# RMSNorm in float32: statistics one group ahead, scaling shared between three engines

## The chip, the cores and the metric

The kernel runs on one core of a Trainium2 chip. The metric is the device time of one execution in microseconds (us). Before the change the median of 12 runs is 162.3 us (162.03 to 162.85).

## What is computed

```python
def setup_inputs():
    batch, seq, dim = 16, 1024, 512
    return {"x": np.random.randn(batch, seq, dim).astype(np.float32),
            "gamma": np.ones(dim, dtype=np.float32)}

def reference(x, gamma):
    eps = 1e-5
    rms = np.sqrt(np.mean(x ** 2, axis=-1, keepdims=True) + eps)
    return (x / rms * gamma).astype(np.float32)
```

There are 16,384 rows of 512 floats. Each row is divided by the root of its mean square and multiplied by gamma. The input is 33.55 MB and the output as much, so 67.1 MB pass between HBM and the on-chip memory, each byte once.

## The kernel before

The rows are cut into four tiles (t = 0 to 3) of 128 partitions x 32 rows. One partition's share of a tile is 32 rows in succession, 64 KB. Three slots in SBUF, `slots[0..2]`, each hold a tile; tile 3 uses slot 0 again. A row is scaled in its slot and stored from there.

All loads and stores are issued from SP, in the order in which the program gives them (lines 47 to 49 and 96 to 116). An issue whose wait is not over holds every later one. The order is written out by hand: the first tile as two loads of 16 rows, tile 1 as one load of 32; then, once the first rows are scaled, three stores of a single row (rows 0, 1 and 2 of tile 0), with loads of 16, 8 and 8 rows of tile 2 between them; then the store of rows 3 to 31 of tile 0; the first half of tile 1; the two loads of tile 3, which need slot 0 to be stored; the second half of tile 1; tile 2 whole; and tile 3 in two halves.

`compute(slot, r0, r1)` (line 64) goes over groups of G = 8 rows. Sums of squares come in two ways, in turn:

- In even groups ACT squares one row at a time (line 78) and gives the row's sum through its accumulator, eight instructions for a group.
- In odd groups ACT squares H = 4 rows at a time into a PSUM tile `sq` (line 72; the pool has two buffers), and DVE reduces it to four sums (line 73), twice for a group.

Then ACT takes the root, with the mean and eps folded in (line 84), DVE the reciprocal (line 85), and DVE scales the eight rows one by one with a SCALAR_TENSOR_TENSOR, row x rstd x gamma (line 87). All four engines run their own queues in order; Tile's scheduler places independent instructions of different groups between each other on each engine. GpSimd (POOL) does nothing but four small memsets. Gamma is spread over the partitions at the start by a matmul with a column of ones into PSUM (line 56), and copied to SBUF as `gamma_b` (line 58).

Of the kernel before, what the change touches and what calls it, by code (L numbers as in the profile page):

```python
# [1 line left out]

# [4 lines left out]


@with_exitstack
def kernel(  # L10
    ctx: ExitStack,
    tc: tile.TileContext,
    x: bass.AP,
    gamma: bass.AP,
    out: bass.AP,
):
    nc = tc.nc
    P = nc.NUM_PARTITIONS
    eps = 1e-5
    fp32 = mybir.dt.float32  # L20
    AF = mybir.ActivationFunctionType
    OP = mybir.AluOpType

    xf = x.flatten_outer_dims()
    of = out.flatten_outer_dims()
    N, D = xf.shape
    R = 32
    G = 8
    H = 4
    assert N == 4 * P * R  # L30

    xv = xf.rearrange("(t p r) d -> t p r d", p=P, r=R)
    ov = of.rearrange("(t p r) d -> t p r d", p=P, r=R)

    const = ctx.enter_context(tc.tile_pool(name="const", bufs=1))
    stats = ctx.enter_context(tc.tile_pool(name="stats", bufs=4))
    psum = ctx.enter_context(tc.tile_pool(name="psum", bufs=2, space=bass.MemoryType.PSUM))

    slots = [const.tile([P, R, D], fp32, name=f"slot{i}") for i in range(3)]

    def load(t, slot, r0, r1):
        nc.sync.dma_start(out=slots[slot][:, r0:r1], in_=xv[t][:, r0:r1])

    def store(t, slot, r0, r1):
        nc.sync.dma_start(out=ov[t][:, r0:r1], in_=slots[slot][:, r0:r1])

    load(0, 0, 0, 16)
    load(0, 0, 16, 32)
    load(1, 1, 0, 32)

    gamma_row = const.tile([1, D], fp32)
    nc.scalar.dma_start(out=gamma_row, in_=gamma.unsqueeze(0))
    ones_col = const.tile([1, P], fp32)
    nc.vector.memset(ones_col, 1.0)  # L54
    gamma_psum = psum.tile([P, H, D], fp32, name="sq")
    nc.tensor.matmul(gamma_psum[:, 0], ones_col, gamma_row, start=True, stop=True)  # L56
    gamma_b = const.tile([P, D], fp32)
    nc.vector.tensor_copy(out=gamma_b, in_=gamma_psum[:, 0])  # L58

    eps_t = const.tile([P, 1], fp32)  # L60
    nc.vector.memset(eps_t, eps)  # L61
    sq_scratch = const.tile([P, D], fp32)

    def compute(slot, r0, r1):
        for g in range(r0, r1, G):
            ss = stats.tile([P, G], fp32, name="ss")
            rms = stats.tile([P, G], fp32, name="rms")
            rstd = stats.tile([P, G], fp32, name="rstd")
            if (g // G) % 2:
                for h in range(0, G, H):  # L70
                    sq = psum.tile([P, H, D], fp32, name="sq")
                    nc.scalar.activation(out=sq, in_=slots[slot][:, g + h : g + h + H, :], func=AF.Square)  # L72
                    nc.vector.tensor_reduce(  # L73
                        out=ss[:, h : h + H], in_=sq, axis=mybir.AxisListType.X, op=OP.add
                    )
            else:
                for r in range(G):
                    nc.scalar.activation(  # L78
                        out=sq_scratch,
                        in_=slots[slot][:, g + r, :],  # L80
                        func=AF.Square,
                        accum_out=ss[:, r : r + 1],
                    )
            nc.scalar.activation(out=rms, in_=ss, func=AF.Sqrt, bias=eps_t, scale=1.0 / D)  # L84
            nc.vector.reciprocal(out=rstd, in_=rms)  # L85
            for r in range(G):
                nc.vector.scalar_tensor_tensor(  # L87
                    out=slots[slot][:, g + r, :],
                    in0=slots[slot][:, g + r, :],
                    scalar=rstd[:, r : r + 1],  # L90
                    in1=gamma_b,
                    op0=OP.mult,
                    op1=OP.mult,
                )

    compute(0, 0, 8)
    store(0, 0, 0, 1)
    load(2, 2, 0, 16)
    store(0, 0, 1, 2)
    load(2, 2, 16, 24)  # L100
    store(0, 0, 2, 3)
    load(2, 2, 24, 32)
    compute(0, 8, 32)
    store(0, 0, 3, 32)
    compute(1, 0, 16)
    store(1, 1, 0, 16)
    load(3, 0, 0, 16)
    load(3, 0, 16, 32)
    compute(1, 16, 32)
    store(1, 1, 16, 32)  # L110
    compute(2, 0, 32)
    store(2, 2, 0, 32)
    compute(0, 0, 16)
    store(3, 0, 0, 16)
    compute(0, 16, 32)
    store(3, 0, 16, 32)


# [1 line left out]
_INS = ['x', 'gamma']  # L120
_OUTS = [((16, 1024, 512), 'float32')]


# [23 lines left out]
```

## Time and profile before

| | us |
|---|---|
| median of 12 runs | 162.3 (162.03 to 162.85) |
| the profiled execution, its own time | 162.34 |
| its span (first to last instruction in the profile) | 160.6 |
| DVE busy | 123.3 (77%), 163 instructions |
| ACT busy | 79.8 (50%), 162 records |
| POOL busy | 0.2 |
| mean transfer rate over the span | 418 GB/s (33.56 MB read, 33.55 MB written) |

Stores were issued from SP at 24.8 us (the first single row), 50.1 (rest of tile 0), 75.1 (first half of tile 1), 132.4 and 147.7 (the halves of tile 3). The loads of tile 3 were issued at 82.0 and 82.4, and landed 19.2 and 28.8 us later.

How to read the views. The page divides the span into 40 slices and gives the busy share of each engine in tenths, and the share of the 16 DMA engines. A table by stage gives, for each stretch, each engine's busy time, the number of its instructions in brackets, the clock, the share of the DMA engines and what they moved; a packet is counted whole in the stretch in which it starts, so a share can stand above 1.00 in a short one. A group of instructions carries its line in the kernel, engine, operation, tiles and shapes, count, then busy time in us and the mean of one in ns, then the idle time before it and what ended it. The list of waits gives who waited for what: us in total, times, longest. In the list of DMA queues, q1 is the queue of SP's loads and stores, q10 that of ACT's load of gamma, and q14 brings instructions; columns are packets, MB and the share of 16 engines' time.

### The profile page before, as it was taken

How to read it: one execution, taken by the hardware profiler on the slowest of the kernel's cores; microseconds unless marked ns; L12 is line 12 of the kernel's file. 1: busy time of each engine (PE TensorE's matmuls, PEld its weight loads, DVE VectorE, ACT ScalarE, POOL GpSimd, SP SyncE). 2: the span in 40 equal slices, each digit the busy share in tenths (PEclk: the TensorE clock that was granted, in tenths of full speed). 3: DMA queues.
4: the chain of work that ended last, by engine and by line, in shares of the span. 5: the costliest groups of instructions: out<-in, count | busy, mean ns of one | idle time of the engine just before them, and what ended most of it. 6: DMA issues, size and time to landing. Idle time of an engine off the chain costs nothing.

```text
span 160.6 us, 414 instructions
## 1 busy us (share of the span) xinstructions
PE 2.0 (1%) x2; PEld 0.5 (0%) x2; DVE 123.3 (77%) x163; ACT 79.8 (50%) x162; POOL 0.2 (0%) x4
## 2 busy tenths in 40 slices
PE   4000000000000000000000000000000000000000
PEld 1000000000000000000000000000000000000000
DVE  0101909999999509999999999998999999998000
ACT  3008999930490999999500934003998960000000
POOL 0000000000000000000000000000000000000000
DMA  7999999969799999998899999999999799799993
GB/s 262 392 400 506 400 408 506 522 261 522 327 394 404 441 445 514 461 459 370 370 441 457 408 425 473 400 433 465 408 514 457 343 506 457 335 392 400 506 400 139
DMA packets 2452, 67.13 MB, mean 418 GB/s; under 512 B 273, under 2 KB 273, under 8 KB 658
## 3 DMA queue, kind: packets, MB, share of 16 engines
q1 hardware_dynamic: 2448, 67.11, 97.7%
q14 instruction: 2, 0.02, 0.0%
q10 hardware_dynamic: 2, 0.00, 0.0%
HBM read 33.56 MB, written 33.55 MB: 418 GB/s over the span
## 4 chain that ended last, share of the span: by engine, by line
DVE 70%; ACT 12%; DMA 8%; issue 2%; DVEq 0%
DVE slot L87 51%; DVE ss L73 18%; DMA slot<-in_x_dram 8%; ACT sq_scratch L78 6%; ACT sq L72 4%; DVE rstd L85 1%; ACT L84 1%; ACT rms L84 1%; DVEq L142 0%
## 5 line engine op out<-in xcount | busy, mean ns | idle before, releaser
L87 DVE SCALAR_TENSOR_TENSOR slot<-slot,rstd,gamma_b 128x512 f32<-128x512 f32 x128 | 85.7, 743 | 0.1
L78 ACT ACTIVATE sq_scratch<-slot 128x512 f32<-128x512 f32 x64 | 40.0, 625 | 14.3 <-DMA slot<-in_x_dram 13.0
L73 DVE TENSOR_REDUCE ss<-sq 128x4 f32<-128x2048 f32 x16 | 36.1, 2268 | 10.3 <-ACT sq L72 10.2
L72 ACT ACTIVATE sq<-slot 128x2048 f32<-128x2048 f32 x16 | 29.8, 1861 | 13.9 <-DVE ss L73 13.9
L84 ACT ACTIVATE rms<-ss,eps_t 128x8 f32<-128x8 f32 x16 | 4.5, 297 | 28.0 <-DVE ss L73 27.7
L78 ACT ACTIVATION_READ_ACCUMULATOR sq_scratch<-slot 128x1 f32 x64 | 11.9, 186 | 0.0
L85 DVE RECIPROCAL rstd<-rms 128x8 f32<-128x8 f32 x16 | 2.9, 190 | 9.8 <-ACT rms L84 9.8
L58 DVE COPY gamma_b<-sq 128x512 f32<-128x512 f32 x1 | 0.7, 692 | 3.4 <-PE sq L56 3.4
L56 PE MATMUL sq<-gamma_row,ones_col 1*128 1x512 f32 x2 | 2.0, 1120 | 2.3 <-DMA gamma_row<-in_gamma_dram 2.3
L78 ACT ACT_TABLE_LOAD x1 | 1.3, 1283 | 1.3 <-PEq L131 1.3
L84 ACT ACT_TABLE_LOAD x1 | 1.3, 1283 | 0.0
L54 DVE MEMSET ones_col<- 1x128 f32 x1 | 0.2, 165 | 0.8 <-PEq L131 0.8
L56 PEld LDWEIGHTS sq<-gamma_row,ones_col 1*128 1x128 f32 x2 | 0.5, 304 | 2.3 <-issue 2.3
L131 POOL MEMSET const-bfloat16-1.0<- 128x1 bf16 x1 | 0.1, 103 | 0.0
L131 POOL MEMSET const-uint8-127<- 128x1 uint8 x1 | 0.1, 103 | 0.0
L131 POOL MEMSET const-float32-1.0<- 128x1 f32 x1 | 0.1, 100 | 0.0
L131 POOL MEMSET const-float32-0.0<- 128x1 f32 x1 | 0.1, 99 | 0.2 <-issue 0.2
L61 DVE MEMSET eps_t<- 128x1 f32 x1 | 0.1, 59 | 0.0
## 6 DMA issues: line engine op xcount, KB each, us to landing
slot<-in_x_dram SPq DMA_DIRECT2D x5, 4096.0 KB, 21.4
out_dram<-slot SPq DMA_DIRECT2D x4, 4096.0 KB, 16.5
out_dram<-slot SPq DMA_DIRECT2D x1, 7424.0 KB, 31.8
slot<-in_x_dram SPq DMA_DIRECT2D x2, 2048.0 KB, 34.6
out_dram<-slot SPq DMA_DIRECT2D x3, 256.0 KB, 23.0
gamma_row<-in_gamma_dram ACTq DMA_DIRECT2D x1, 2.0 KB
slot<-in_x_dram SPq DMA_DIRECT2D x1, 40.6
out_dram<-slot SPq DMA_DIRECT2D x1, 23.3
```

The costliest lines, as they stand in the source:

```text
L54: nc.vector.memset(ones_col, 1.0)
L56: nc.tensor.matmul(gamma_psum[:, 0], ones_col, gamma_row, start=True, stop=True)
L58: nc.vector.tensor_copy(out=gamma_b, in_=gamma_psum[:, 0])
L61: nc.vector.memset(eps_t, eps)
L72: nc.scalar.activation(out=sq, in_=slots[slot][:, g + h : g + h + H, :], func=AF.Square)
L73: nc.vector.tensor_reduce(out=ss[:, h : h + H], in_=sq, axis=mybir.AxisListType.X, op=OP.add)
L78: nc.scalar.activation(out=sq_scratch, in_=slots[slot][:, g + r, :], func=AF.Square, accum_out=ss[:, r : r + 1],)
L84: nc.scalar.activation(out=rms, in_=ss, func=AF.Sqrt, bias=eps_t, scale=1.0 / D)
L85: nc.vector.reciprocal(out=rstd, in_=rms)
L87: nc.vector.scalar_tensor_tensor(out=slots[slot][:, g + r, :], in0=slots[slot][:, g + r, :], scalar=rstd[:, r : r + 1], in1=gamma_b, op0=O ...
L131: nc = _bacc.Bacc("TRN2", target_bir_lowering=False, num_devices=1)
```

## The change

- The sums of all groups are made in one way: ACT squares four rows at a time, the first four of a group into PSUM (`sq0`), the last four into SBUF (`sq4`), one buffer each; DVE reduces both (`sum_squares`).
- The sums of group k + 1 are written in the program ahead of the scaling of group k (`apply`), and its root and reciprocal (`inverse_rms`) behind it.
- Scaling is shared. ACT scales the first four rows of a group by rstd with a Copy each; POOL then multiplies the four by gamma in one TENSOR_TENSOR of 128x2048. DVE scales the last four as before, but takes gamma from PSUM (`gamma_psum`) in place of SBUF.
- The first load, 16 rows, becomes two of 8 rows. All other transfers are issued in the same order; they stand in `transfers`, called behind each group.
- At the start, ACT and DVE get an `addr_align(128, offset=60, max_nops=0)`: the instruction that follows is placed at slot 60 of a stretch of 128 instruction slots, and the padding is branched over.

In the order of instructions on the engines: DVE has 64 SCALAR_TENSOR_TENSOR in place of 128, and 32 TENSOR_REDUCE in place of 16; ACT has 32 Squares, 64 Copies and 16 roots in place of 64 + 16 Squares and 16 roots; POOL has 16 TENSOR_TENSOR, and one more ISA instruction ahead of them (a reload of library code). On SP there is one issue more.

```diff
+    nc.scalar.addr_align(128, offset=60, max_nops=0)
+    nc.vector.addr_align(128, offset=60, max_nops=0)
...
-    psum = ctx.enter_context(tc.tile_pool(name="psum", bufs=2, space=bass.MemoryType.PSUM))
+    psum = ctx.enter_context(tc.tile_pool(name="psum", bufs=1, space=bass.MemoryType.PSUM))
...
-    load(0, 0, 0, 16)
+    load(0, 0, 0, 8)
+    load(0, 0, 8, 16)
...
-    gamma_psum = psum.tile([P, H, D], fp32, name="sq")
-    nc.tensor.matmul(gamma_psum[:, 0], ones_col, gamma_row, start=True, stop=True)
-    gamma_b = const.tile([P, D], fp32)
-    nc.vector.tensor_copy(out=gamma_b, in_=gamma_psum[:, 0])
+    gamma_psum = psum.tile([P, D], fp32, name="gamma_psum")
+    nc.tensor.matmul(gamma_psum, ones_col, gamma_row, start=True, stop=True)
+    gamma_b = const.tile([P, 1, D], fp32)
+    nc.vector.tensor_copy(out=gamma_b[:, 0], in_=gamma_psum)
...
-    sq_scratch = const.tile([P, D], fp32)
-    def compute(slot, r0, r1):
...
+    def sum_squares(slot, g):
+        ss = stats.tile([P, G], fp32, name="ss")
+        for h, home in ((0, psum), (H, const)):
+            sq = home.tile([P, H, D], fp32, name=f"sq{h}")
+            nc.scalar.activation(out=sq, in_=slots[slot][:, g + h : g + h + H, :], func=AF.Square)
+            nc.vector.tensor_reduce(out=ss[:, h : h + H], in_=sq, axis=mybir.AxisListType.X, op=OP.add)
+        return ss
+    def inverse_rms(ss):
+        rms = stats.tile([P, G], fp32, name="rms")
+        rstd = stats.tile([P, G], fp32, name="rstd")
+        nc.scalar.activation(out=rms, in_=ss, func=AF.Sqrt, bias=eps_t, scale=1.0 / D)
+        nc.vector.reciprocal(out=rstd, in_=rms)
+        return rstd
+    def apply(slot, g, rstd):
+        x = slots[slot]
+        for r in range(H):
+            nc.scalar.activation(
+                out=x[:, g + r, :], in_=x[:, g + r, :], func=AF.Copy, scale=rstd[:, r : r + 1]
+            )
+        nc.gpsimd.tensor_tensor(
+            out=x[:, g : g + H, :],
+            in0=x[:, g : g + H, :],
+            in1=gamma_b.to_broadcast([P, H, D]),
+            op=OP.mult,
+        )
+        for r in range(H, G):
+            nc.vector.scalar_tensor_tensor(
+                out=x[:, g + r, :],
+                in0=x[:, g + r, :],
+                scalar=rstd[:, r : r + 1],
+                in1=gamma_psum,
+                op0=OP.mult,
+                op1=OP.mult,
+            )
+    groups = [(t, g) for t in range(4) for g in range(0, R, G)]
+    slot_of = [0, 1, 2, 0]
+    def transfers(t, g):
...
+        elif (t, g) == (0, 24):
+            store(0, 0, 3, 32)
+        elif (t, g) == (1, 8):
+            store(1, 1, 0, 16)
+            load(3, 0, 0, 16)
+            load(3, 0, 16, 32)
...
+    rstd = inverse_rms(sum_squares(0, 0))
+    for k, (t, g) in enumerate(groups):
+        more = k + 1 < len(groups)
+        if more:
+            tn, gn = groups[k + 1]
+            ss = sum_squares(slot_of[tn], gn)
+        apply(slot_of[t], g, rstd)
+        if more:
+            rstd = inverse_rms(ss)
+        transfers(t, g)
```

## The prediction

> **What bounds the kernel now.** I read the page's share lines first: which resource is full, not which engine is busiest.
>
> ```profile
> span 160.6 us, 414 instructions
> ...
> DMA  7999999969799999998899999999999799799993
> ...
> q1 hardware_dynamic: 2448, 67.11, 97.7%
> q14 instruction: 2, 0.02, 0.0%
> ...
> DVE 70%; ACT 12%; DMA 8%; issue 2%; DVEq 0%
> ```
>
> The queue of loads and stores keeps 16 DMA engines at work for 97.7% of 160.6 us, 156.9 us. The chain of waits names DVE at 70%; that is a trap. It follows whoever released the last store, and says nothing of whether the transfers were idle meanwhile. The stage table tells that:
>
> ```profile
> core 0: us, PE busy (x) PEld busy (x) DVE busy (x) ACT busy (x) POOL busy (x), PEclk, DMA share, GB/s
> 1.73:148.10 146.37, 2.04 (x2) 0.49 (x2) 123.10 (x161) 79.31 (x162) 0.00 (x0) 1.00 1.00 430
> 147.50:148.00 0.50, 0.00 (x0) 0.00 (x0) 0.22 (x1) 0.00 (x0) 0.00 (x0) 1.00 0.46 197
> 148.00:148.50 0.50, 0.00 (x0) 0.00 (x0) 0.00 (x0) 0.00 (x0) 0.00 (x0) 1.00 0.16 66
> 148.50:149.00 0.50, 0.00 (x0) 0.00 (x0) 0.00 (x0) 0.00 (x0) 0.00 (x0) 1.00 2.29 983
> 157.00:157.50 0.50, 0.00 (x0) 0.00 (x0) 0.00 (x0) 0.00 (x0) 0.00 (x0) 1.00 2.28 983
> 157.50:158.00 0.50, 0.00 (x0) 0.00 (x0) 0.00 (x0) 0.00 (x0) 0.00 (x0) 1.00 0.00 0
> 158.00:158.50 0.50, 0.00 (x0) 0.00 (x0) 0.00 (x0) 0.00 (x0) 0.00 (x0) 1.00 0.17 66
> 158.50:160.60 2.10, 0.00 (x0) 0.00 (x0) 0.00 (x0) 0.00 (x0) 0.00 (x0) 1.00 0.00 0
> ```
>
> From the first packet to 148.1 the share is 1.00. A packet counts in the slice where it starts, so short slices count packets: 983 GB/s in 0.5 us is 492 KB, fifteen rows of 32 KB. Fifteen engines start their last packet in 157.0 to 157.5, and one in 158.0 to 158.5: a straggler. A packet takes 2.28 x 16 x 0.5 / 15 = 1.22 us, so it ends at about 159.2. Fifteen of sixteen first packets of the last store start in 148.5 to 149.0: that store was issued as its last row was scaled at 147.7, and engines that were empty at about 148.2 waited some 0.2 to 0.4 us. The straggler did not wait: its packet records, chained end to start, show no gap from 1.9 to 159.2. So the end is 1.7 us of head, the straggler's own packets, and 1.4 us behind its last one.
>
> ```profile
> SPq L45 <- DVE slot L87: 95.4, 6, 30.6
> ...
> SPq L42 <- DMA out_dram<-slot: 6.4, 1, 6.4
> ```
>
> SP waits 95.4 us for scaled rows, but it is merely early: its queue is full behind it.
>
> What delays the straggler? In two slices, from 45.9 and from 65.3, one instruction fetch each:
>
> ```profile
> q14 instruction: 1, 0.01, 19.3%
> ```
> ```profile
> q14 instruction: 1, 0.01, 9.7%
> ```
>
> 19.3% of 16 engines over 0.1 us is 0.31 us, 9.7% over 0.2 us the same: one 8 KB packet on one engine. In the chained records the fetch at 65.4 lies on the straggler, and the data packet behind it took 0.38 us more than its like. Together 0.69 us, and the straggler is last by 0.64 (159.23 against 158.59).
>
> [...]
>
> **The change, part by part**, against the profiled execution: 162.34 us, of which 160.6 span and 1.74 around it; the median is 162.3, so a difference carries over.
>
> ```profile
> L87 DVE SCALAR_TENSOR_TENSOR slot<-slot,rstd,gamma_b 128x512 f32<-128x512 f32 x128 | 85.7, 743 | 0.1
> L78 ACT ACTIVATE sq_scratch<-slot 128x512 f32<-128x512 f32 x64 | 40.0, 625 | 14.3 <-DMA slot<-in_x_dram 13.0
> L73 DVE TENSOR_REDUCE ss<-sq 128x4 f32<-128x2048 f32 x16 | 36.1, 2268 | 10.3 <-ACT sq L72 10.2
> L72 ACT ACTIVATE sq<-slot 128x2048 f32<-128x2048 f32 x16 | 29.8, 1861 | 13.9 <-DVE ss L73 13.9
> ```
>
> DVE: 64 of the 128 scalings go; at 85.7/128 = 0.67 us that is -42.9. Sixteen more reductions: 16 x 2.26 = +36.1. The 64 that stay read gamma from PSUM[...]. Sum -3 us: DVE stays near 120 us, 7.5 per group of eight rows[...].
>
> ACT: 64 single-row Squares with their accumulator reads go, -(40.0 + 11.9); sixteen four-row Squares come, +29.8; 64 Copies come with a per-row scale[...]. About 100 us, 6.5 per group: below DVE.
>
> POOL: sixteen multiplies of 128x2048 at 4.5 us, 72 us. Bounds: 2.3, DVE's row for as many elements[...].
>
> Are these ever late? A store must be issued before the bytes queued ahead run out, at 67.11/156.9 = 0.428 MB/us from 1.7. Ahead of rows 3 to 31 of tile 0 lie 25.95 MB: limit 62. Half tile 1: 80; tile 2: 119; tile 3: 139 and 149. Before, they went at 50.1, 75.1, about 117, 132.4 and 147.7: the last was the tight one. After: tile 1 lands at 1.7 + 40.6 = 42.3, its first sums reach DVE 1.9 later, and twelve groups of 7.5 end at 134; the last POOL multiply adds at most 4.5, so the last store goes by about 139, nine ahead of need. Tile 3's second half lands at 82.4 + 28.8 = 111.2 as before: two groups, 15, plus 4 of sums and 4.5 of POOL: 135, no later. Running ahead queues the next group's Squares and reductions before the scaling, and the wait of each Square for its one buffer holds Copies behind it on ACT; the nine us cover it.
>
> So compute worth: nothing. The straggler never waited for it; the 0.2 to 0.4 us at 148 belong to other engines. Stores leave SP in the same order, and now wait for POOL as well; the loads of tiles 2 and 3 stand behind them in SP's queue, so a late POOL would hold them too. The first Sqrt is placed behind the third four-row Square, so group 0 waits for rows 8 to 15 (about 13 us) and two table loads: its first store goes at about 25, as before (24.8); it is needed by 41. The copy of gamma and the memsets are over by 5 us, before any row has landed. Splitting the first load: 16 KB packets took 611 ns, 32 KB ones 1213, so 2 x 611 - 1213 = 9 ns for eight pairs per engine, +0.07 us. The earlier start of group 0 (about 8 instead of 12.8) hides behind 39 us of queued loads.
>
> The alignment: [...] If each body then lies within one block, the fetch moves to the start, before the first data packet at 1.73, and the straggler gains 0.69; the next engine then ends last, 0.64 earlier, and 0.07 is added: 0.57. If a boundary is still crossed, nothing. A gain also needs the next engine not to be delayed. Bounds: -0.7 and +0.3 (a third fetch).
>
> POOL's queue gets one more ISA instruction ahead of its first multiply, a reload of library code. [...] I take 0 for the forecast and keep 1.0 for a case of its own. [...]
>
> **Rivals and forecast.**
> 1. Fetches leave the stretch, straggler gone: 162.3 - 0.57 = 161.7. Chance 0.42.
> 2. The change does nothing: DMA floor kept, fetches still cross the data: 162.3 + 0.07 = 162.4. For it: a floor at 97.7%, and two engines still running some 120 instructions each. 0.33.
> 3. Library code or more fetches on the same 16 engines: +1.0, 163.3; 0.3 to 2.5 possible. 0.15.
> 4. Slower: POOL and DVE exclude each other[...]. Place: the four scalings beside each multiply. Price: 7.5 + 4.5 = 12 per group, 44 + 12 x 12 = 188, plus 11.8 for the last store and 2.8 behind: 203. It decides once a group takes over (147.7 - 4.5 - 44.2)/12 = 8.25 us; partial blocking at 9 gives +9. 0.10.
>
> I forecast the first. A measurement tells about 0.2% (0.32 us) from no change. Of case 1, 0.04 is within that; of case 2, 0.02 on each side: faster 0.40, same 0.33, slower 0.27. Range 161.4 to 163.4: cases 1 and 2 and the cheaper half of 3.
>
> **What would show it.** Right: DMA share 1.00 from 1.7 to about 157.5, no dip at 148, last store issued before 143, no q14 packet inside, no lone packet in the last slice, span near 160.0. Two q14 packets and a straggler again: case 2. Packets of another queue at the start: case 3. DMA slices at zero late, SP's last waits on POOL past 147: case 4.

## The result

The changed kernel takes 164.75 us (median; 164.32 to 164.98), the kernel before 162.27 (161.91 to 162.85 over the runs beside it and the experiments). The ratio is 1.0149, interval 1.0138 to 1.0160: slower by 2.5 us, and outside the predicted range. The profiled execution took 164.67 with a span of 162.9 (before: 162.34 and 160.6), so the loss lies inside the span.

The page of the changed kernel first, the share lines and the busy times:

```profile
span 162.9 us, 360 instructions
...
PE 2.0 (1%) x2; PEld 0.5 (0%) x2; DVE 115.6 (71%) x115; ACT 105.2 (65%) x114; POOL 72.5 (45%) x20
...
DMA  6999899997999999999899999998996996999960
...
q1 hardware_dynamic: 2592, 67.11, 96.4%
q14 instruction: 4, 0.03, 0.1%
...
DMA 42%; DVE 24%; ACT 10%; issue 3%; POOLq 3%; POOL 3%; ACTq 0%; SPq 0%
```

The same 67.11 MB pass; 96.4% of 162.9 is 157.0 us, and before it was 156.9. So the transfers did not take more engine time in sum. What is new stands in two places: four instruction fetches instead of two, and the last digit of the DMA row, 0 where it was 3. The stage table shows that end:

```profile
core 0: us, PE busy (x) PEld busy (x) DVE busy (x) ACT busy (x) POOL busy (x), PEclk, DMA share, GB/s
1.73:158.00 156.27, 2.04 (x2) 0.49 (x2) 115.41 (x113) 105.18 (x114) 72.32 (x16) 1.00 1.00 429
157.00:157.50 0.50, 0.00 (x0) 0.00 (x0) 0.00 (x0) 0.00 (x0) 0.00 (x0) 1.00 0.45 197
157.50:158.00 0.50, 0.00 (x0) 0.00 (x0) 0.00 (x0) 0.00 (x0) 0.00 (x0) 1.00 0.31 131
158.00:158.50 0.50, 0.00 (x0) 0.00 (x0) 0.00 (x0) 0.00 (x0) 0.00 (x0) 1.00 0.01 0
158.50:159.00 0.50, 0.00 (x0) 0.00 (x0) 0.00 (x0) 0.00 (x0) 0.00 (x0) 1.00 0.00 0
159.00:159.50 0.50, 0.00 (x0) 0.00 (x0) 0.00 (x0) 0.00 (x0) 0.00 (x0) 1.00 0.15 66
159.50:160.00 0.50, 0.00 (x0) 0.00 (x0) 0.00 (x0) 0.00 (x0) 0.00 (x0) 1.00 0.00 0
160.00:160.50 0.50, 0.00 (x0) 0.00 (x0) 0.00 (x0) 0.00 (x0) 0.00 (x0) 1.00 0.15 66
160.50:162.90 2.40, 0.00 (x0) 0.00 (x0) 0.00 (x0) 0.00 (x0) 0.00 (x0) 1.00 0.00 0
```

66 GB/s over 0.5 us is one packet of 32 KB. In 159.0 to 159.5 one packet starts, and in 160.0 to 160.5 one more: a single engine works off its last two alone. The packet records do not name the engine; here and below a packet is put on the engine whose packet before it ends where this one starts. That leaves an uncertainty of up to 0.2 us in the figures that compare engines. By these records the late engine ends 159.7 us after the first data packet; the other fifteen are done by 157.1. Before, the straggler ended 157.5 after the first packet, the next engine 156.9. The mean share from the first packet to 158 is 1.00 as it was before; the median engine ends 156.4 after the first packet, before it was 156.7. One engine lost 2.2 us, not the sixteen.

Where the fetches lie in the changed kernel: the list of queues over 0 to 5 us, and then over 60 to 80 us, each line with packets, MB and the share of 16 engines.

```profile
q1 hardware_dynamic: 70, 1.15, 66.9%
q14 instruction: 2, 0.02, 1.1%
```
```profile
q14 instruction: 2, 0.02, 0.2%
```

The records put them at 1.76 (ACT's) and 3.76 us (DVE's), and at 67.97 (DVE's) and 69.96 (ACT's). The first data packet starts at 1.73. So the early fetch of DVE falls among data that already flow, and the one in the middle is still there. One fetch is one packet of 8 KB. In the chained records both of DVE's fetches lie on one DMA engine, the one that ends last; ACT's do not lie on it.

The compute side came out as forecast. The groups:

```profile
L88 POOL TENSOR_TENSOR slot<-slot,gamma_b 128x2048 f32<-128x2048 f32 x16 | 72.3, 4523 | 66.3 <-ACT slot L85 64.6
L72 DVE TENSOR_REDUCE ss<-sq 128x4 f32<-128x2048 f32 x32 | 71.3, 2266 | 9.1 <-ACT sq L71 9.0
L71 ACT ACTIVATE sq<-slot 128x2048 f32<-128x2048 f32 x32 | 59.9, 1883 | 9.3 <-DMA slot<-in_x_dram 7.6
L85 ACT ACTIVATE slot<-slot,rstd 128x512 f32<-128x512 f32 x64 | 40.8, 709 | 12.1 <-DVE rstd L79 12.1
L95 DVE SCALAR_TENSOR_TENSOR slot<-slot,rstd,gamma_psum 128x512 f32<-128x512 f32 x64 | 43.5, 739 | 0.2
```

And the timeline of SP's issues (start, length, how many):

```profile
85.88 53.58 SPq L48 DMA_DIRECT2D out_dram<-slot  x4
```

The last of these four stores is issued at 85.88 + 53.58 = about 139.5, against 147.7 before. Eight microseconds of lead at the last store are real, and worth nothing.

### The profile page after: what moved, and what is told of

It reads as the page before. It is cut to its first block, busy times and chain, and to the rows that moved or that the text cites. A ratio compares the mean times of both kernels' runs of the same rounds, so it can differ in the third digit from the quotient of the medians.

```text
span 162.9 us, 360 instructions
## 1 busy us (share of the span) xinstructions
PE 2.0 (1%) x2; PEld 0.5 (0%) x2; DVE 115.6 (71%) x115; ACT 105.2 (65%) x114; POOL 72.5 (45%) x20
## 3 DMA queue, kind: packets, MB, share of 16 engines
q1 hardware_dynamic: 2592, 67.11, 96.4%
## 4 chain that ended last, share of the span: by engine, by line
DMA 42%; DVE 24%; ACT 10%; issue 3%; POOLq 3%; POOL 3%; ACTq 0%; SPq 0%
DMA out_dram<-slot 23%; DMA slot<-in_x_dram 20%; DVE ss L72 15%; DVE slot L95 8%; ACT sq L71 5%; ACT slot L85 4%; POOLq L165 3%; POOL slot L88 3%; ACT L78 1%; DVE rstd L79 0%; ACTq L165 0%; SPq L45 0%; ACT rms L78 0%; ACTq L71 0%; POOLq L88 0%
## 5 line engine op out<-in xcount | busy, mean ns | idle before, releaser
L88 POOL TENSOR_TENSOR slot<-slot,gamma_b 128x2048 f32<-128x2048 f32 x16 | 72.3, 4523 | 66.3 <-ACT slot L85 64.6
L72 DVE TENSOR_REDUCE ss<-sq 128x4 f32<-128x2048 f32 x32 | 71.3, 2266 | 9.1 <-ACT sq L71 9.0
L71 ACT ACTIVATE sq<-slot 128x2048 f32<-128x2048 f32 x32 | 59.9, 1883 | 9.3 <-DMA slot<-in_x_dram 7.6
L85 ACT ACTIVATE slot<-slot,rstd 128x512 f32<-128x512 f32 x64 | 40.8, 709 | 12.1 <-DVE rstd L79 12.1
L95 DVE SCALAR_TENSOR_TENSOR slot<-slot,rstd,gamma_psum 128x512 f32<-128x512 f32 x64 | 43.5, 739 | 0.2
L62 DVE COPY gamma_b<-gamma_psum 128x512 f32<-128x512 f32 x1 | 0.7, 692 | 8.4 <-PE gamma_psum L60 8.4
L60 PE MATMUL gamma_psum<-gamma_row,ones_col 1*128 1x512 f32 x2 | 2.0, 1120 | 7.9 <-DMA gamma_row<-in_gamma_dram 7.9
L60 PEld LDWEIGHTS gamma_psum<-gamma_row,ones_col 1*128 1x128 f32 x2 | 0.5, 304 | 7.9 <-issue 7.9
```

Of the source, the lines that this page charges most:

```text
L60: nc.tensor.matmul(gamma_psum, ones_col, gamma_row, start=True, stop=True)
L62: nc.vector.tensor_copy(out=gamma_b[:, 0], in_=gamma_psum)
L72: nc.vector.tensor_reduce(out=ss[:, h : h + H], in_=sq, axis=mybir.AxisListType.X, op=OP.add)
L85: nc.scalar.activation(out=x[:, g + r, :], in_=x[:, g + r, :], func=AF.Copy, scale=rstd[:, r : r + 1])
L88: nc.gpsimd.tensor_tensor(out=x[:, g : g + H, :], in0=x[:, g : g + H, :], in1=gamma_b.to_broadcast([P, H, D]), op=OP.mult,)
L95: nc.vector.scalar_tensor_tensor(out=x[:, g + r, :], in0=x[:, g + r, :], scalar=rstd[:, r : r + 1], in1=gamma_psum, op0=OP.mult, op1=OP.mult,)
```

## The experiments

Times are medians; the time of the kernel before is that of the same set of runs. "From the first packet" is the last packet's end less the first data packet's start in the profiled run. The theories go by letters in the expectations below, which say what each of them forecasts. Every kernel here computes the whole output.

### Is it the alignment or the work?

e1_no_align takes the two alignments out of the changed kernel and keeps everything else; e2_before_aligned puts them, alone, into the kernel before.

```diff
-    nc.scalar.addr_align(128, offset=60, max_nops=0)
-    nc.vector.addr_align(128, offset=60, max_nops=0)
```

> The changed kernel without its two alignment lines. Theory F (the alignment): it makes ACT and DVE branch over padding, which adds two instruction fetches in the first 4 us, one of them on the DMA engine that ends last; without it two q14 packets are left, the last engine trails by under 1 us, and the time is 162.3 (161.7 to 162.6). Theory W (the work: POOL's multiplies and the reload of its library, the split of the first load, or the new order slow one DMA engine): the lone late engine stays and the time is 164.4 to 164.9.

Measured: 162.62 against 162.37, ratio 1.0010 (0.9997 to 1.0024).

> The kernel before with the two alignment lines added and nothing else. Theory F: fetches in the first 4 us and again near the middle, an engine that trails by 2 to 3 us, time 164.0 to 165.0. Theory W: no change, 162.1 to 162.6.

Measured: 164.40, ratio 1.0129 (1.0115 to 1.0142). The two lines alone cost 2.0 of the 2.5 us, with the old order of work and without a library reload or a split load; all the rest of the change together cannot be told from nothing. In the records of e2 fourteen engines wait 0.5 to 1.3 us near 148 for the last store, which leaves SP 0.8 us later than in the kernel before; the late engine does not wait there and ends 2.1 us behind the next. The page of e1:

```profile
span 160.6 us, 357 instructions
...
DMA  6999999969799999998899999999999799799993
...
q1 hardware_dynamic: 2592, 67.11, 97.7%
q14 instruction: 2, 0.02, 0.0%
```

Its stage table at the end:

```profile
157.00:157.50 0.50, 0.00 (x0) 0.00 (x0) 0.00 (x0) 0.00 (x0) 0.00 (x0) 1.00 0.91 393
157.50:158.00 0.50, 0.00 (x0) 0.00 (x0) 0.00 (x0) 0.00 (x0) 0.00 (x0) 1.00 0.16 66
158.00:158.50 0.50, 0.00 (x0) 0.00 (x0) 0.00 (x0) 0.00 (x0) 0.00 (x0) 1.00 0.01 0
158.50:160.60 2.10, 0.00 (x0) 0.00 (x0) 0.00 (x0) 0.00 (x0) 0.00 (x0) 1.00 0.00 0
```

The lone packets after 159 are gone, and so are the two early fetches: two are left, both between 40 and 80 us. The last packet ends 157.5 us after the first, as before.

### Which of the two lines?

e3_align_act keeps only ACT's line in the changed kernel, e4_align_dve only DVE's.

> The changed kernel with the alignment of ACT alone. In the profile of the change the fetch at 3.76 us, after which ACT's first table load starts, lies on the late engine, that at 1.76 us elsewhere. Theory F with ACT's fetch as the culprit: 164.2 to 164.9. With DVE's as the culprit: 162.0 to 162.8. Theory W: 164.4 to 164.9 here and in the next run.

Measured: 162.57, ratio 1.0023 (1.0012 to 1.0034). I had put the loss down to ACT's early fetch; that falls. What ACT's line does cost is small: the interval of the ratio overlaps that of e1, which has neither line. The last packet ends 157.9 after the first, but on the engine of DVE's fetch at 59.5 us; up to that fetch no engine of e3 is over 0.2 us behind the median.

> The changed kernel with the alignment of DVE alone. Theory F with ACT's fetch as the culprit: 162.0 to 162.8, one fetch in the first 4 us on an engine that does not end last. With DVE's: 164.2 to 164.9. Theory W: 164.4 to 164.9.

Measured: 164.74, ratio 1.0148 (1.0129 to 1.0168), the ratio of the full change. It is DVE's line. Its early fetch takes 0.31 us, and the packet behind it some 0.53 more: 0.84 us, a third of the loss. The rest had to come from somewhere.

### Does a small early delay grow?

In the records of the changed kernel the late engine loses more at certain places, and only there: at its last load packets before the other engines go over from the packets of a load to those of the store queued behind it (about 40, 51, 57 and 63 us), and at the fetch at 67.97. Hence the theory that a delay grows at each such change. e6_dve_slot0 asks for slot 0 on DVE alone: the fetch at the start stays, the one in the middle goes.

```diff
-    nc.scalar.addr_align(128, offset=60, max_nops=0)
-    nc.vector.addr_align(128, offset=60, max_nops=0)
+    nc.vector.addr_align(128, offset=0, max_nops=0)
```

> The changed kernel with DVE alone aligned, to slot 0: a jump to the next boundary, and its some 125 instructions then lie in one stretch, so no DVE fetch near 68 us. It parts the early fetch from the middle one. Theory G (the early delay grows with the transfers that follow, and is most of the loss): 163.8 to 164.4, the middle fetch being worth its 0.3 to 0.7. Theory S (each fetch costs the same 0.3 to 0.8, the loss is their sum): 163.0 to 163.4.

Measured: 164.29, ratio 1.0142 (1.0125 to 1.0159), as the growing delay has it. This run has the cleanest chain of packets. How far the late engine is behind the median of the others when as many bytes are through (worked out from the packet records):

```
time of the late engine, us   11.4  19.3  35.0  43.8  51.7  60.4  76.9  160.8
behind by, us                 0.97  1.00  1.01  2.00  1.95  2.60  2.60   2.60
```

The fetch at 3.83 with the packet behind it gives 0.84 of the first microsecond. The next comes near 40 us, where tile 1's load ends, the last 0.6 by 60, where the single-row stores and the loads of tile 2 change places. No second fetch of DVE, and from 60 on nothing is lost or made good. In e1 the same measure is 0 up to its fetch at 59, then 0.6, and 1.06 from the change at 109 to the end; in the kernel before 0.7 after its fetch at 65.4, 1.1 from 109, and 0.8 at the end, since most of the others wait at 148. The changed kernel ends at 3.3: e6's 2.6 and the middle fetch's 0.66.

Not every change adds to the delay. At 109 us the late engine loses nothing in the changed kernel and in e6, where it is 3.3 and 2.6 us behind; an engine that is 0.7 to 1.6 us behind loses 0.4 to 0.7 there (before, e1, e3, e5). No run shows what makes the difference.

e5_slot76 asks for slot 76 on both engines: no fetch at all in the first 4 us, DVE's at 55.7.

```diff
-    nc.scalar.addr_align(128, offset=60, max_nops=0)
-    nc.vector.addr_align(128, offset=60, max_nops=0)
+    nc.scalar.addr_align(128, offset=76, max_nops=0)
+    nc.vector.addr_align(128, offset=76, max_nops=0)
```

> The changed kernel with both alignments to slot 76 in place of 60. With no alignment (first call) DVE's fetch came at 59.2 us, with slot 60 at 67.9, eight or nine DVE instructions later; so DVE's body begins by itself near slot 69, ACT's near 62, both just past 60, and slot 60 can only be had in the next stretch of 128, across a boundary. Theory J (the jump across the boundary fetches early): slot 76 lies ahead in the same stretch, no fetch in the first 4 us, the middle one a little earlier (about 50 us): 162.3 to 163.2. Theory B (any branch over padding costs a fetch): fetches in the first 4 us and 164.2 to 164.9.

Measured: 163.36 against 162.12, ratio 1.0085 (1.0061 to 1.0110): without the early fetch nearly half of the loss is gone, but a bit more stays than I had expected. The fetch now falls ahead of the changes at 63 and 108 us, where the records show its engine falling back by another 0.6 and 0.7. In four kernels with the single-row stores in which DVE fetches once, the time falls as that fetch comes later: 164.29 at 3.8 us (e6), 163.36 at 55.7 (e5), 162.62 at 59.2 (e1), 162.3 at 65.4 (before).

### Is it the fetch, or any early delay of one engine?

e7_early_row and e8_late_row leave the alignments out, and give one engine 16 KB more of data: one partition's first eight rows of tile 2, loaded right behind the first load (they are loaded again later), or eight rows of tile 1 loaded once more near the end, into a slot that is no longer used.

```diff
     load(0, 0, 0, 8)
+    nc.sync.dma_start(out=slots[2][0:1, 0:8], in_=xv[2][0:1, 0:8])
```
```diff
     store(2, 2, 0, 32)
+    nc.sync.dma_start(out=slots[1][0:1, 16:24], in_=xv[1][0:1, 16:24])
```

> The changed kernel without alignment, and one load of one partition more (16 KB, eight rows of tile 2 that are loaded again later), issued behind the first load: 0.6 us on one DMA engine in the first microseconds, with no instruction fetch in it. Theory G: the delay of that engine grows along the run, 163.5 to 165.0, a late engine by 1.5 to 3 us. Theory S: the engine has slack or ends 0.6 us later, 162.3 to 163.1.

Measured: 163.35, ratio 1.0063 (1.0045 to 1.0081), runs from 162.15 to 164.11: just under the band of the growing delay, and widely scattered. In the profiled run the engine with the extra row lost another 1.0 us at 62.4, and ended 2.0 us behind the median engine.

> The same 16 KB on one engine, but late: issued on SP behind the store of tile 2, so behind every change from loads to stores (into slot 1, whose rows have been stored). Theory G: nothing is left to make it grow, 162.3 to 163.1. Theory S: the same as the run with the early row, within 0.2%.

Measured: 162.50, ratio 1.0030 (1.0018 to 1.0042). The same bytes cost more when they come early. The times alone do not decide it: the late row fell on an engine that had room, ended 0.5 us behind the median, about its own 0.6, and was done before the engine of DVE's fetch (156.9 against 157.6 from the first packet). The early row also fell on an engine without a DVE fetch; there its 0.6 us, with 0.4 more in the first packets, became 2.0. So the direction is that of a delay that grows; the size is not settled, since the early row cost less than the early fetch.

### Are the single-row stores what it grows on?

e9_aligned_no_rows takes the three single-row stores out of the changed kernel, e10_no_align_no_rows out of e1, e11_before_no_rows out of the kernel before; each stores tile 0 whole instead.

```diff
-            store(0, 0, 0, 1)
...
-            store(0, 0, 1, 2)
...
-            store(0, 0, 2, 3)
...
-            store(0, 0, 3, 32)
+            store(0, 0, 0, 32)
```

> The changed kernel, alignment kept, without the three stores of single rows among the loads of tile 2; rows 0 to 2 go with the rest of tile 0 as one store of 32 rows. Three changes from loads to stores, at about 42, 52 and 57 us, are gone; those at about 61 and 109 stay. Theory G: the late engine has fewer places to fall further behind; 163.4 to 164.2, and the late engine's last packet of the load of tile 1 takes no longer than the others'. Theory S: only the small packets are saved, 24 of 84 ns on each engine less the 76 ns that a row costs in a long packet, 0.2 us: 164.5 to 164.8.

Measured: 163.76 against 162.06, ratio 1.0102 (1.0081 to 1.0123). Fewer changes between loads and stores, and a third of the loss goes. The records agree: behind the early fetch the late engine stays 0.7 to 0.9 us back up to 60 us, so it loses nothing where the single rows stood; it loses 0.65 at the one change at 60, another 0.66 at its middle fetch, and ends 2.15 behind.

> The same without the alignment. In the trace of the change all engines lose some 0.4 us in their last packets of tile 1's load, ahead of the first single row; if the change from loads to stores is what costs that, it goes, with 0.2 us of small packets: 161.6 to 162.1, faster than the kernel before. If a change from loads to stores costs the same wherever it is made, only the small packets are saved: 162.1 to 162.5.

Measured: 162.04, ratio 0.9999 (0.9984 to 1.0013): no gain that can be told, at the border of the two expected bands. The records show why none was to be had: the load packets ahead of the one change left, at 58 to 61 us, took 0.8 and 0.4 us more on the mean of the engines, where with the single rows the change at 39 cost 0.45 and the others little. The cost of the change was moved and not removed.

> The kernel before with the single-row stores taken out in the same way. As for the run above: 161.6 to 162.1 where the changes between loads and stores cost, 162.1 to 162.4 where only packets do. Slower than either would mean that the last store, which here is issued just as the queue runs dry, comes later.

Measured: 162.34, ratio 1.0021 (1.0009 to 1.0034). In the old kernel too, nothing to gain; it is 0.3 us slower. Its profiled run was its slowest (163.57), and there the engine with a fetch at 46.3 fell back by 0.6 at 60 and 0.6 at 110 and ended 2.1 us behind: without any alignment, the delay behind a later fetch grew as well. That a waiting issue holds the later ones on SP shows in e11: with no store ahead of them all six first loads were issued in 0.73 to 3.77 us, where before those of tile 2 went at 25.23 to 27.17, each behind a single-row store.

### The aligned code with the fetch out of the way

e12_aligned_held keeps both lines at slot 60, but holds the loads until ACT has written one element of each row of the three slots (the loads overwrite them), so that the early fetches are over before a data packet starts. e13_held has the same hold without the alignments.

```diff
+    held = const.tile([P, R], fp32)
+    nc.vector.memset(held, 0.0)
+    for i in range(3):
+        nc.scalar.activation(out=slots[i][:, :, 0], in_=held, func=AF.Copy)
     load(0, 0, 0, 8)
```

> The changed kernel, alignment kept, with all loads held until ACT has written one element of each row of the three slots (the loads overwrite them): the data starts only when ACT's table load is over, near 5 us, so both early fetches fall ahead of the first packet (about 6 us in place of 1.7). Theory F with G (an early fetch costs because the data is already flowing, and its delay grows): no engine trails by more than about 1.5 us, and the time is that without alignment, 162.4 to 162.6, plus the 4.2 us of the later start: 166.4 to 167.0. Theory X (the jump costs something else, such as a slower DMA queue for the whole run): 164.75 plus 4.2, 168.7 to 169.2.

Measured: 166.94 against 162.18, ratio 1.0284. The hold itself costs more than it could save, as it must; what counts is the time from the first data packet. Its stage table, and the line of fetches in the queue list of 0 to 5.9 us:

```profile
0.00:5.90 5.90, 1.42 (x2) 0.49 (x2) 0.22 (x3) 1.78 (x4) 0.20 (x4) 1.00 0.01 3
5.90:162.00 156.10, 0.62 (x1) 0.00 (x0) 115.42 (x113) 103.97 (x113) 72.33 (x16) 1.00 1.00 430
162.00:162.50 0.50, 0.00 (x0) 0.00 (x0) 0.00 (x0) 0.00 (x0) 0.00 (x0) 1.00 0.00 0
162.50:163.00 0.50, 0.00 (x0) 0.00 (x0) 0.00 (x0) 0.00 (x0) 0.00 (x0) 1.00 0.16 66
```
```profile
q14 instruction: 2, 0.02, 1.0%
```

The first data packet starts at 6.2, and the last lone packet starts in 162.5 to 163.0: 157.7 us from first to last, against 159.7 in the changed kernel. With the same placement of code, the loss is gone once the early fetch does not meet the data. That queue list has both fetches and no data packet yet. The late engine here keeps up with the others until its middle fetch at 66.3.

> The same hold without the alignment: ACT's table load ends near 2.5 us, the first packet starts near 3.7, 2.0 us later than without the hold. Both theories: 162.5 plus 2.0, 164.2 to 164.8. It gives what the hold itself costs, so that the run above is compared by the time from its first packet.

Measured: 165.18, ratio 1.0183 (1.0161 to 1.0204), a little above what I expected: 158.2 from the first packet. Its DVE fetch came at 57.6, 53.8 after its first packet (in e5 54.0), ahead of the same changes as in e5; its engine lost 0.4 and 0.7 at them.

## Why the prediction was wrong

- *A DMA floor, compute worth nothing*: right. e1 has all of the new work and takes the old time (ratio 1.0010). DVE was busy 115.6 us (forecast about 120), ACT 105 (about 100), POOL 16 x 4.52 = 72 (72). What the forecast took for ACT's Copies, and POOL's 4.5 us, were estimates that no row of the profile before shows; a Copy took 709 ns, 64 of them 40.8 us, and a multiply 4523 ns. The last store went at about 139 as forecast. One detail was off: the copy of gamma, forecast by 5 us, came at 10: ACT's issue of the load of gamma lasted 2.39 us with its early fetch (in e4, which has no such fetch, 0.51, and the copy came at 4.2); gamma was first used at 21 us, so this cost nothing.
- *More time for gamma in PSUM*: not seen. The row is 739 ns against 743 before. The profile before gives 123.3 - 42.9 + 36.1 = 116.5 us for DVE; what the forecast of about 120 has beyond that was my estimate for gamma in PSUM, which no trace showed. It is most of DVE's difference.
- *The 0.2 to 0.4 us at 148 belong to other engines*: right, though by the chained records eleven engines waited, and 0.07 to 0.52 us. In e1 the median engine ends 156.5 us after the first packet, before it was 156.7; the last one ends at 157.5 in both.
- *Splitting the load +0.07, library reload 0*: within e1's interval (162.62 against 162.37), together. DMA packets of a reload are not seen in the list of queues.
- *POOL and DVE exclude each other (203 us)*: did not happen; 46 of DVE's 64 scalings lay wholly within a multiply of POOL, and took 738 ns on the mean, against 740 for the seven that met no multiply at all.
- *The alignment*: this is the step that failed: "If each body then lies within one block, the fetch moves to the start, before the first data packet at 1.73, and the straggler gains 0.69". Nothing in the profile before showed that the alignment would do so; it was an estimate, with a block taken as a stretch of 128 slots. None of its three parts came true. The trace has a branch on ACT and one on DVE at 0.7 to 0.8 us; DVE's early fetch came at 3.76, after the first data. The middle fetch stayed, at 67.97 us against 59.2 in e1, eight or nine DVE instructions later. From that I estimate that DVE's code would begin near slot 69 of its stretch anyway, already past slot 60, so that it was moved forward by most of a stretch and crossed the next boundary again. Slot 76 without an early fetch (e5), and slot 0 without a middle fetch of DVE (e6), fit this estimate. And the straggler lost where it should have gained: the bound of +0.3 for a third fetch took the delay for the packet's own length. It measured 0.31 + 0.53 us on the engine, and 2.4 us at the end (e4 against its runs of before).
- *Rival 3*, "more fetches on the same 16 engines", named the right kind of cost with the wrong size: 1.0 us, chance 0.15. Its upper bound of 2.5 us is what was measured, but by luck: it was an estimate for the library code, which no trace showed, and which cost nothing that e1 could tell.

What the runs showed in place of the failed step: a fetch of DVE that met the data, with the packet behind it, delayed one engine by 0.69 us before (at 65.4) and by 0.84 and 0.66 in the changed kernel (at 3.76 and 67.97); in e6 the delay of that engine grew at changes from loads to stores that followed, from 1.01 us at 35.0 to 2.60 at 60.4; and the changed kernel ended with its last engine, 159.7 us after the first packet, with the other fifteen done by 157.1.

That the early fetch is the cause is shown by e1, e2, e4, e6 and e12. That the delay grows at the changes is read from the packet records of several runs and agrees with e6, e7 and e9; it does not grow at all of them (109 us). Why the last load packets of a lagging engine are slower is not shown. Open as well are the scatter of e7 and why e5 and e13 stand a bit above what I expected. No version was faster than the kernel before by more than its interval; the best was e10, 162.04, ratio 0.9999.

## What to carry to other kernels

In a kernel that the transfers bound, compare the engines' last packets, not only the mean share: here it was 1.00 from 1.73 to 158 us with one engine two packets behind. Moving code moved the instruction fetches (DVE's from 59.2 us in e1 to 3.76 and 67.97), and a fetch that fell early among the data cost several times its own length (0.31 us became 2.4); see where the code stands and where its fetches fall before placing it anew, and look whether the first data packet is ahead of it. Work taken off engines that only run ahead of the transfers brought nothing here (e1, 162.62 against 162.37).

## What was not expected of the hardware

- An 8 KB fetch of DVE took 0.31 us, but the data packet behind it lost another 0.35 to 0.53 us (0.38 before, 0.53 and 0.35 in the changed kernel). Behind ACT's fetches of 0.31 us it lost 0.25 (before, at 45.9) and 0.12 (in the changed kernel, at 69.96); ACT's early one, at 1.76, took 0.54 itself.
- DVE's and ACT's early fetches went to different DMA engines, and ACT's cost little where DVE's cost 2.4 us (157.9 us from first to last packet in e3, 159.6 in e4, 157.5 before). ACT's came at 1.76 us, with the first data packets, and left no delay: in the changed kernel no engine but that of DVE's fetches is over 0.35 us behind the median from 6 to 58 us. DVE's came at 3.76. Whether the moment makes the difference is not shown: no run has a fetch of ACT at that later moment.
- The last load packets of tile 1, ahead of the first single-row store (about 39 us), took 0.34 to 0.55 us more on all 16 engines before than the 2.42 us of their like. In the changed kernel it was 0.01 to 0.47 us on fifteen engines and 0.79 on the late one; in e6, at 39.9 us, it was up to 1.4 us on the one already behind.
